# Other PSUM banks for the second weight tile of a down-projection, and one queue for most of the last stores

## The chip, the cores and the metric

The kernel runs on one core of a Trainium2 chip. The core has five engines with a queue each: TensorE (PE, with a separate row PEld for its weight loads), VectorE (DVE), ScalarE (ACT), GpSimd (POOL) and SyncE (SP). TensorE writes its products into PSUM, which has eight banks of 128 x 512 float32 here; VectorE and ScalarE read them from there. Transfers between the main memory and SBUF are issued by SyncE, ScalarE or GpSimd. The metric is the device time of one execution in microseconds (us). The kernel before took 1692.35 us, the median of 3 runs (1691.88 to 1692.66).

## The reference

A decoder trunk of two layers on 512 tokens of width 1024, in float32. Each layer is a half-weighted SwiGLU, a mixer (sliding-window attention beside a short convolution) and a second half-weighted SwiGLU:

```
def swiglu(h, w_gate, w_up, w_down):
    return (jax.nn.silu(h @ w_gate) * (h @ w_up)) @ w_down
...
    for l in range(DEPTH):
        x = x + 0.5 * swiglu(rms_norm(x, ffn1_norm[l]), ffn1_wg[l], ffn1_wu[l], ffn1_wd[l])
        h = rms_norm(x, mix_norm[l])
        z = h @ w_in[l]
...
        x = x + jnp.concatenate([attn_out, conv_out], axis=-1) @ w_out[l]
        x = x + 0.5 * swiglu(rms_norm(x, ffn2_norm[l]), ffn2_wg[l], ffn2_wu[l], ffn2_wd[l])
    return rms_norm(x, final_norm)
```

The inner width of a SwiGLU (D_FF) is 2816, which is eleven blocks of 256 columns.

## The kernel before

**Precision.** Every operand is split into a high and a low part in a shorter float type, and a product is three matmuls: high x high, high x low, low x high. A weight tile arrives as `raw`, ScalarE casts it to `wh` (line 198), and VectorE subtracts to get `wl` (line 199). Where a split is marked "far" (`split_far`, lines 201 to 205), ScalarE writes both `wl = -raw` and `wh`, and a GpSimd transfer adds `raw` to `wl` (line 205), so VectorE has nothing to do with it.

**An FFN in blocks.** `ffn` (from line 758) goes through a list of stages. In three of the four FFNs the list is INNER or LAST: first "p", block 0 done plainly; then "d" for block 0, its down-projection; then "w" for blocks 1, 3, 5 and so on, two blocks at a time by a Winograd-like scheme with seven products instead of eight (`winograd2`, line 861); then "s", the down-projections of most of those blocks by the same scheme (`share`, line 720). The first FFN of the kernel has the list FIRST, which begins with two plain blocks.

**The residual.** The stream x is kept transposed, as eight tiles `xs[c]` of 128 features by 512 tokens. `down` (line 304) yields for each c a sum `acc` in PSUM, and VectorE adds it: `xs[c] += 0.5 * acc` (line 990). Block 0 has two chunks of 128 inner columns, so `abreast` gives 4: one weight tile holds the columns for four c. Of the first weight tile (c = 0 to 3) the four groups are made side by side by `level` (line 290), where `fresh` is set, that is in the three FFNs with the lists INNER and LAST; the last matmuls of its four groups (line 299) follow each other. Of the second weight tile (c = 4 to 7) each group is made on its own by `group` (line 263, matmuls in lines 273, 276 and 280), with six matmuls.

**PSUM banks.** `psum` (line 92) gives out the eight banks under three names: four "mm", two "sc", two "aux". A tile of a name waits until the one that had its bank before has been read. `level` takes all four mm banks, and so does the second weight tile after it. In the Winograd stages, whose seven steps are listed in CHAINS (line 52), the sum x uses mm from step 0 on, w uses aux at step 1, and y uses sc at step 3. Before block 0, sc and aux hold sums of the mixer or of the FFN before, and aux the sum of squares for the norm (line 484). In the last FFN, `Finale.step` (line 1010) turns x back to tokens after the steps 0, 1 and 2 of block 1, through sc, sc, and mm and aux.

**The end.** `Finale.down` (line 1090) makes the last block's down-projection with tokens on the partitions: for each of four token tiles t and two column halves h a product, the residual add (line 1069), the sum of squares on ScalarE (line 1071), and when both halves are in, the inverse root (lines 1077 and 1082, Newton's step in lines 398 to 400). Then `scale` (line 1109) multiplies each half and stores it: h = 1 on VectorE with a store from SyncE's queue, h = 0 on ScalarE with a store from ScalarE's own queue (line 1118). The last token tile's second half is made in two pieces of 256 columns. From token tile 2 on, the order of ScalarE and VectorE is as written (`manual_schedule`, line 1132).

**Order elsewhere.** Where no `manual_schedule` stands, a planner orders each engine's instructions from modelled durations, with the order of the program as priority, and adds the waits.

Of the kernel before, what the change touches and what calls it, by code (L numbers as in the profile page):

```python
# [15 lines left out]
P = 128  # L16
D = 1024
S = 512
# [5 lines left out]
KC = D // P  # L24
NT = S // P
# [33 lines left out]
def trunk_kernel(  # L59
# [23 lines left out]
    nc = tc.nc  # L83
# [8 lines left out]
    def psum(tag, shape, name):  # L92
        return ps.tile(shape, F32, tag=tag, bufs={"mm": 4, "sc": 2, "aux": 2}[tag], name=name)

    def g2(name, dt=F32, shape=(P, S)):
        return work.tile(list(shape), dt, tag="g2", bufs=14, name=name)
# [15 lines left out]
    def small(name, n=NT, dt=F32):  # L112
        return work.tile([P, n], dt, tag="small", bufs=16, name=name)
# [54 lines left out]
    order = []  # L168
# [88 lines left out]
    def take_split():  # L257
        n = state["group"]
        state["group"] += 1
        need_split(n + SPLIT_AHEAD if n else 0)  # L260
        return n, *split_of.pop(n)

    def group(rhs, between=None, own=None, order=range(KC)):

        n, hi, lo = own or take_split()
        acc = psum("mm", [P, S], f"acc_{n}")
        order = order[: len(rhs)]
        first, last = order[0], order[-1]
        late = n in (1, 2, 3)
        for k in order:  # L270
            if between:
                between(k, hi, lo)
            nc.tensor.matmul(acc, hi[:, k, :], rhs[k][0], start=k == first, stop=False)  # L273
            if n == 0:
                nc.tensor.matmul(acc, lo[:, k, :], rhs[k][0], start=False, stop=False)
            nc.tensor.matmul(  # L276
                acc, hi[:, k, :], rhs[k][1], start=False, stop=n == 0 and k == last
            )
            if n != 0 and not late:
                nc.tensor.matmul(acc, lo[:, k, :], rhs[k][0], start=False, stop=k == last)  # L280
        if late:
            for k in order:
                nc.tensor.matmul(acc, lo[:, k, :], rhs[k][0], start=False, stop=k == last)
        return acc

    def abreast(kc):

        return max(1, KC // kc) if kc in (2, 4) else 1

    def level(n, hi, lo, rhs, wide):  # L290

        accs = [psum("mm", [P, S], f"acc_{n}_{j}") for j in range(wide)]
        cols = [slice(j * P, (j + 1) * P) for j in range(wide)]
        for k, (xh, xl) in enumerate(rhs):
            for j in range(wide):
                nc.tensor.matmul(accs[j], hi[:, k, cols[j]], xh, start=k == 0, stop=False)
                nc.tensor.matmul(accs[j], lo[:, k, cols[j]], xh, start=False, stop=False)
            for j in range(wide):
                nc.tensor.matmul(
                    accs[j], hi[:, k, cols[j]], xl, start=False, stop=k + 1 == len(rhs)  # L300
                )
        return accs

    def down(rhs, fresh=False):

        wide = abreast(len(rhs))
        for c in range(0, KC, wide):
            n, hi, lo = take_split()
            if fresh and c == 0:
                yield from enumerate(level(n, hi, lo, rhs, wide))  # L310
                continue
            for j in range(wide):
                cols = slice(j * P, (j + 1) * P)
                yield c + j, group(rhs, own=(f"{n}_{j}", hi[:, :, cols], lo[:, :, cols]))

    def plan():
        def cols(src, k0, kc, n, how=None):
# [84 lines left out]
    class Norm:  # L402
# [65 lines left out]
        def groups(self, n, accs=()):  # L468

            accs = list(accs) or [group(self.h, order=self.order)]  # L470
            parts = self.parts()
            while len(accs) < n:
                at, step = (1, 2) if self.i else (3, 2)
                due = len(accs) == at
                accs.append(
                    group(self.h, lambda k, hi, lo: due and k == step and self.factors(parts))
                )
            return accs
# [279 lines left out]
    def ffn(norm, stages, after=None, late=None):  # L758
# [192 lines left out]
        for i, (what, b) in enumerate(stages):  # L951
# [33 lines left out]
            for c, acc in down(rhs, b == (0,) and not first):  # L985
                if b == (0,):
                    made = {0: "t3", 4: "t1"} if first else {0: "b21", 2: "t2", 5: "t3"}
                    if c in made:
                        norm.make(made[c])
                nc.vector.scalar_tensor_tensor(  # L990
                    xs[c], acc, 0.5, xs[c], op0=ALU.mult, op1=ALU.add
                )
                flush()
                if final:
                    after(c)
# [5 lines left out]
    class Finale:  # L1001
# [88 lines left out]
        def down(self, rhs):  # L1090
            for half in range(2):
                gb = g2(f"gain_{half}")
                nc.sync.dma_start(
                    gb, final_norm[half * S : (half + 1) * S].partition_broadcast(P)
                )
                self.gain.append(gb)
            done = small("done", NT)
            self.widen(0, len(rhs) // 2)
            for t in range(NT):
                rest = done[:, t : t + 1]  # L1100
                acc = self.products(rhs, 0, t, 0, S)
                self.close(acc, 0, t, 0, rest)
                nc.vector.tensor_scalar(rest, rest, 1.0 / D, EPS, op0=ALU.mult, op1=ALU.add)
                if t == 0:
                    self.widen(1, len(rhs) // 2)
            def factor(t, ssq):
                return self.root(t, ssq, done[:, t : t + 1])

            def scale(t, by, h):
                y = self.y[t][h]  # L1110
                if h:
                    nc.vector.scalar_tensor_tensor(
                        y, y, by, self.gain[h], op0=ALU.mult, op1=ALU.mult
                    )
                else:
                    nc.scalar.activation(y, y, AF.Copy, scale=by)
                cols = slice(h * S, (h + 1) * S)
                (nc.sync if h else nc.scalar).dma_start(out[0, t * P : (t + 1) * P, cols], y)

            def piece(t, c0, wide):  # L1120
                ssq = small(f"ssq_end{t}_{c0}", 1)
                self.close(self.products(rhs, 1, t, c0, wide), 1, t, c0, ssq)
                return ssq

            for t in range(NT - 2):
                by = factor(t, piece(t, 0, S))
                for h in (1, 0):
                    scale(t, by, h)


            a, b = NT - 2, NT - 1
            with tc.manual_schedule(engines={act, dve}):
                ssq = piece(a, 0, S)
                early = self.guess(a, ssq, done[:, a : a + 1])
                first = piece(b, 0, H)
                by = self.mend(a, ssq, done[:, a : a + 1], early)
                scale(a, by, 0)
                second = piece(b, H, H)
                scale(a, by, 1)
                rest = done[:, b : b + 1]  # L1140
                nc.vector.scalar_tensor_tensor(
                    rest, first, 1.0 / D, rest, op0=ALU.mult, op1=ALU.add
                )
                by = self.mend(b, second, rest, self.guess(b, second, rest))
                for h in (1, 0):
                    scale(b, by, h)
# [233 lines left out]
```

## Time and profile before

| | |
|---|---|
| median of 3 runs | 1692.35 us |
| profiled execution | 1690.47 us |
| its span, from the first to the last instruction | 1688.6 us |
| granted TensorE clock | 0.999 |
| busy: TensorE, VectorE, ScalarE, GpSimd | 1675.1, 1382.8, 967.7, 215.3 us |
| moved by transfers | 284.19 MB |

The rows come from one profiled execution. A row of the timeline has the start and the duration in us, the engine, the line of the kernel, the operation, the tile written and the tiles read, the shapes, how often the row stands for (x2: two in a row), and in brackets the idle time of the engine before it with what ended it. A matmul of 512 columns is shown with 0.39 us, but the next starts before it ends, so its rate is read from starts. ACTq and SPq are the queues of ScalarE and SyncE; their rows are the issues of transfers.

### The profile page before, as it was taken

How to read it: one execution, taken by the hardware profiler on the slowest of the kernel's cores; microseconds unless marked ns; L12 is line 12 of the kernel's file. 1: busy time of each engine (PE TensorE's matmuls, PEld its weight loads, DVE VectorE, ACT ScalarE, POOL GpSimd, SP SyncE). 2: the span in 40 equal slices, each digit the busy share in tenths (PEclk: the TensorE clock that was granted, in tenths of full speed). 3: DMA queues.
4: the chain of work that ended last, by engine and by line, in shares of the span. 5: the costliest groups of instructions: out<-in, count | busy, mean ns of one | idle time of the engine just before them, and what ended most of it. 6: DMA issues, size and time to landing. Idle time of an engine off the chain costs nothing.

```text
span 1688.6 us, 23567 instructions
## 1 busy us (share of the span) xinstructions
PE 1675.1 (99%) x9014; PEld 1443.3 (85%) x9014; DVE 1382.8 (82%) x1817; ACT 967.7 (57%) x1335; POOL 215.3 (13%) x192
## 2 busy tenths in 40 slices
PE   9999999999999999999999999999999999999998
PEld 6888889988898888889988888999888988888886
DVE  7987679988799967799798677997787997667995
ACT  6545565466566655564465555644555766556654
POOL 1011111001221111111011111110013111111111
PEclk9999999999999999999999999999999999999999
DMA  8467787731597677778466777785226867777881
GB/s 250 104 171 189 186 199 187 188 100 51 135 215 167 174 183 186 187 191 221 150 144 179 187 186 183 198 202 156 63 63 143 219 137 195 184 183 185 224 213 51
DMA packets 191846, 284.19 MB, mean 168 GB/s; under 512 B 9004, under 2 KB 77684, under 8 KB 191732
## 3 DMA queue, kind: packets, MB, share of 16 engines
q1 hardware_dynamic: 151108, 199.95, 37.7%
q0 software_dynamic: 39472, 81.27, 28.6%
q8 instruction: 71, 1.16, 0.3%
q10 hardware_dynamic: 1152, 1.45, 0.2%
q14 instruction: 43, 0.35, 0.1%
HBM read 261.14 MB, written 2.10 MB: 156 GB/s over the span
## 4 chain that ended last, share of the span: by engine, by line
PE 93%; DVE 3%; DMA 2%; issue 1%; POOL 0%; ACT 0%; SPq 0%; ACTq 0%; POOLq 0%; DVEq 0%
PE x L711 25%; PE y L711 12%; PE x_s L696 8%; PE acc L273 7%; PE acc L276 7%; PE acc L280 7%; PE w L711 6%; PE y_s L696 4%; PE x_s L711 3%; PE w_s L696 2%; PE x_m L696 2%; PE at L917 2%; PE y_m L696 1%; PE y_s L711 1%; DMA wl<-raw 1%
## 5 line engine op out<-in xcount | busy, mean ns | idle before, releaser
L198 ACT CAST wh<-raw 128x1024 fp32r<-128x1024 f32 (+1 forms) x482 | 505.2, 1048 | 531.0 <-PE x L711 132.0
L199 DVE TENSOR_TENSOR wl<-raw,wh 128x1024 fp32r<-128x1024 f32 (+1 forms) x481 | 588.4, 1225 | 210.3 <-ACT wh L198 208.3
L273 PE MATMUL acc<-xh,wh 128*128 128x512 f32 x448 | 176.5, 394 | 0.1
L276 PE MATMUL acc<-xl,wh 128*128 128x512 f32 x448 | 175.5, 392 | 0.1
L280 PE MATMUL acc<-xh,wl 128*128 128x512 f32 x416 | 162.5, 391 | 0.0
L193 POOL DMA_DIRECT2D raw<-in_ffn_wu_dram x39 | 47.3, 1217 | 531.6 <-DMA raw<-in_ffn_wu_dram 306.8
L276 PEld LDWEIGHTS acc<-xl,wh 128*128 128x128 f32 x448 | 84.2, 188 | 18.5 <-DVE xl L421 1.7
L273 PEld LDWEIGHTS acc<-xh,wh 128*128 128x128 f32 x448 | 84.2, 188 | 17.1 <-issue 0.5
L280 PEld LDWEIGHTS acc<-xh,wl 128*128 128x128 f32 x416 | 78.1, 188 | 16.2
L193 POOL DMA_DIRECT2D raw<-in_ffn_wg_dram x39 | 47.2, 1249 | 228.0 <-DMA raw<-in_ffn_wu_dram 100.0
L223 DVE TENSOR_TENSOR raw<-raw,raw 128x1024 f32<-128x1024 f32 x58 | 70.9, 1229 | 6.3 <-DMA wl<-raw 5.7
L193 POOL DMA_DIRECT2D raw<-in_ffn_wd_dram x32 | 38.6, 1206 | 260.6 <-DMA raw<-in_ffn_wd_dram 142.4
L711 PE MATMUL w<-wh,fb21h 128*128 128x512 f32 x152 | 60.7, 399 | 0.0
L711 PE MATMUL x<-wh,ft2h 128*128 128x512 f32 x152 | 60.6, 398 | 0.0
L711 PE MATMUL y<-wh,ft3h 128*128 128x512 f32 x152 | 60.4, 398 | 0.0
L711 PE MATMUL w<-wl,fb21h 128*128 128x512 f32 x152 | 59.4, 391 | 0.0
L711 PE MATMUL x<-wl,ft2h 128*128 128x512 f32 x152 | 59.3, 390 | 0.0
L711 PE MATMUL y<-wh,ft3l 128*128 128x512 f32 x152 | 59.2, 390 | 0.0
L711 PE MATMUL y<-wl,ft3h 128*128 128x512 f32 x152 | 59.2, 390 | 0.0
L711 PE MATMUL w<-wh,fb21l 128*128 128x512 f32 x152 | 59.2, 389 | 0.0
L711 PE MATMUL x<-wl,fb11h 128*128 128x512 f32 x152 | 59.2, 389 | 0.0
L711 PE MATMUL x<-wh,fb11h 128*128 128x512 f32 x152 | 59.1, 389 | 0.0
(503 smaller groups left out, 4805.0 us busy)
## 6 DMA issues: line engine op xcount, KB each, us to landing
raw<-in_ffn_wu_dram SPq DMA_DIRECT2D x127, 512.0 KB, 4.3
raw<-in_ffn_wd_dram SPq DMA_DIRECT2D x104, 512.0 KB, 5.0
raw<-in_ffn_wg_dram SPq DMA_DIRECT2D x87, 512.0 KB, 5.0
raw<-in_ffn_wu_dram POOLq DMA_DIRECT2D x39, 512.0 KB, 8.0
raw<-in_ffn_wg_dram POOLq DMA_DIRECT2D x39, 512.0 KB, 6.0
raw<-in_w_in_dram SPq DMA_DIRECT2D x36, 512.0 KB, 3.6
raw<-in_ffn_wd_dram POOLq DMA_DIRECT2D x32, 512.0 KB, 8.4
raw<-raw POOLq DMA_DIRECT2D x20, 512.0 KB, 7.2
```

The source lines that it names most:

```text
L193: nc.gpsimd.dma_start(out=r, in_=rows_of(*more), accum_op=ALU.add)
L198: nc.scalar.copy(hi, raw)
L199: eng.tensor_sub(lo, raw, f32(hi))
L223: nc.vector.tensor_add(a11, a11, s1)
L273: nc.tensor.matmul(acc, hi[:, k, :], rhs[k][0], start=k == first, stop=False)
L276: nc.tensor.matmul(acc, hi[:, k, :], rhs[k][1], start=False, stop=n == 0 and k == last)
L280: nc.tensor.matmul(acc, lo[:, k, :], rhs[k][0], start=False, stop=k == last)
L696: nc.tensor.matmul(accs[c // 2][:, c % 2, :], w[:, k, cols], x_[:, 2 * h + k, :], start=start and c % 2 == 0 and h + k + i == 0, stop=h + ...
L711: nc.tensor.matmul(accs[u], x_[:, 2 * h + k, tok], w[:, k, :], start=start and h + k + i == 0, stop=h + k == 2 and i == 2, skip_group_chec ...
L917: nc.tensor.transpose(tp[:, t * P : (t + 1) * P], ups[t][:, c * P : (c + 1) * P], ident)
```

## The change

The groups of the second weight tile (c = 4 to 7) of block 0, in the FFNs where the first weight tile goes through `level`, write to the banks sc, sc, aux and aux in place of the four mm banks. And at the end the h = 0 stores of the token tiles 0 to 2 are issued by SyncE in place of ScalarE; the last token tile's stays with ScalarE.

```
-    def group(rhs, between=None, own=None, order=range(KC)):
+    def group(rhs, between=None, own=None, order=range(KC), tag="mm"):
 
         n, hi, lo = own or take_split()
-        acc = psum("mm", [P, S], f"acc_{n}")
+        acc = psum(tag, [P, S], f"acc_{n}")
...
                 cols = slice(j * P, (j + 1) * P)
-                yield c + j, group(rhs, own=(f"{n}_{j}", hi[:, :, cols], lo[:, :, cols]))
+                own = (f"{n}_{j}", hi[:, :, cols], lo[:, :, cols])
+                tag = ("sc", "sc", "aux", "aux")[j] if fresh else "mm"
+                yield c + j, group(rhs, own=own, tag=tag)
...
                 cols = slice(h * S, (h + 1) * S)
-                (nc.sync if h else nc.scalar).dma_start(out[0, t * P : (t + 1) * P, cols], y)
+                queue = nc.scalar if h == 0 and t == NT - 1 else nc.sync
+                queue.dma_start(out[0, t * P : (t + 1) * P, cols], y)
```

## The prediction

> **What bounds the kernel now.** I read the page's engine table first.
>
> ```profile
> span 1688.6 us, 23567 instructions
> PE 1675.1 (99%) x9014; PEld 1443.3 (85%) x9014; DVE 1382.8 (82%) x1817; ACT 967.7 (57%) x1335; POOL 215.3 (13%) x192
> ```
>
> TensorE works 1675.1 of 1688.6 us, so 13.5 us in all is idle, the start and the tail included. A change that leaves the matmuls alone can only win from those 13.5 us. The waits of TensorE come next, first those of the matmuls, then those of the weight loads (columns: total us, times, longest).
>
> ```profile
> PE acc L273 <- DVE x L990: 1.9, 3, 0.7
> PE x_m L696 <- DVE wl L199: 0.9, 2, 0.5
> PEld acc L273 <- DVE x L990: 3.2, 3, 1.1
> ```
>
> The longest wait of the matmuls is on the line that the change touches: a group's first matmul (L273) waits for the residual add that empties its bank (L990), three times, once for each of the three FFNs whose block 0 goes through `level`. The timeline of TensorE at the three places shows what one wait costs.
>
> ```profile
> 538.25 1.07 PE L299 MATMUL acc<-a,wh 128*128 128x512 f32 x4
> 540.00 0.50 PE L273 MATMUL acc<-a,wh 128*128 128x512 f32 x1 [0.68 <-DVE x L990]
> 540.34 0.39 PE L276 MATMUL acc<-a,wh 128*128 128x512 f32 x1
> ...
> 874.29 1.07 PE L299 MATMUL acc<-a,wh 128*128 128x512 f32 x4
> 875.92 0.50 PE L273 MATMUL acc<-a,wh 128*128 128x512 f32 x1 [0.56 <-DVE x L990]
> ...
> 1372.84 1.07 PE L299 MATMUL acc<-a,wh 128*128 128x512 f32 x4
> 1374.59 0.50 PE L273 MATMUL acc<-a,wh 128*128 128x512 f32 x1 [0.68 <-DVE x L990]
> ```
>
> Four matmuls take 1.07 us and one 0.39, so they start (1.07 - 0.39) / 3 = 0.227 us apart. Unhindered, L273 would start at 538.25 + 4 x 0.227 = 539.16 and L276 at 539.39; L276 starts at 540.34. The first wait costs 0.95 us: 0.84 of delay and 0.11 because the restarted matmul takes 0.34 to its successor instead of 0.227. The second costs 875.92 - 875.20 + 0.11 = 0.83, the third 1374.59 - 1373.75 + 0.11 = 0.95. **Together 2.73 us**, between the 1.9 and the 3.2 of the two wait lists.
>
> **Part one: the banks.** No instruction is added or removed; groups 4 to 7 of the down-projection write sc, sc, aux, aux instead of waiting for the four mm banks. The old tenants of those banks (the mixer's sums in both, then the squared sum in aux, all read while the block's own products run) are gone by then, so the wait falls away. What is late next? VectorE and two transfers, which do not come earlier because TensorE does.
>
> ```profile
> 538.00:567.00 29.00, 28.32 (x125) 23.12 (x124) 28.97 (x32) 17.91 (x21) 1.21 (x1) 1.00 0.51 123
> ...
> 565.78 2.35 DVE L199 TENSOR_TENSOR wl<-raw,wh 128x1024 fp32r<-128x1024 f32 x2
> 568.45 1.23 DVE L199 TENSOR_TENSOR wl<-raw,wh 128x1024 fp32r<-128x1024 f32 x1 [0.31 <-ACT wh L198]
> ...
> 567.57 0.19 PEld L711 LDWEIGHTS x<-wl,ft1h 128*128 128x128 f32 x1
> ```
>
> The first row is the window after the first wait: length, then busy time of PE, PEld, DVE. VectorE is busy 28.97 of 29.00 us, so it cannot deliver sooner than it does now. The split that it makes last in this stretch (the first of two, done at 565.78 + 1.22 = 567.00) is loaded at 567.57: 0.57 us of room. TensorE, 0.95 us earlier, would run into it and keep about 0.57. (The signal costs some hundredths and the quicker restart after a wait gives 0.11 back; I let them cancel.) The other splits of that stretch have over 1.1 us of room, by the same subtraction.
>
> ```profile
> 872.56 1.42 POOL L205 DMA_DIRECT2D wl<-raw  x1
> DMA to landing us min/median/max: 8.6/8.6/8.6
> 881.73 0.19 PEld L711 LDWEIGHTS x<-wl,fb11h 128*128 128x128 f32 x1
> ...
> 1369.87 0.90 POOL L205 DMA_DIRECT2D wl<-raw  x1
> DMA to landing us min/median/max: 7.6/7.6/7.6
> 1380.39 0.19 PEld L711 LDWEIGHTS x<-wl,fb11h 128*128 128x128 f32 x1
> ```
>
> At the second place the limit is the weight whose low part is made by a transfer. It is issued at 872.56, before the wait, and lands 8.6 us later at 881.16; the load is at 881.73. Again 0.57 us of room against a gain of 0.83, so about 0.57 is kept. At the third place the same transfer lands at 1369.87 + 7.6 = 1377.47 and is loaded at 1380.39: 2.9 us of room. VectorE's splits have about as much there, since the final stage's transposes stretch TensorE's steps, so the whole 0.95 is kept. Sum: 0.57 + 0.57 + 0.95 = **2.1 us** kept. The ends: with the room as it stands or smaller by a tenth for rounding, 1.9; with nothing in the way, 2.73. I take 2.1, because both rooms are read from rows. Right behind, VectorE idles again and waits for ScalarE's cast (the row of 568.45), and the casts and the loads wait for buffers that TensorE frees, so what is kept travels to the end.
>
> The new tenants must leave in time too.
>
> ```profile
> 545.67 1.88 DVE L990 SCALAR_TENSOR_TENSOR x<-acc,x 128x512 f32<-128x512 f32 x3
> ...
> 551.18 5.44 PE w L711 x24
> ```
>
> The last add of the eight ends at 545.67 + 1.88 = 547.55. The next user of the aux banks is w, from 551.18 (550.2 if TensorE is 0.95 earlier): 2.7 us of cover. The next user of the mm banks, x, finds them emptied earlier than before.
>
> A rule of the Trainium skill speaks against a gain here: the page "TensorE: Matmul & The Clock Gate", section "HAM oscillation — how this bites in real kernels", reports of a thin-M kernel that double-buffering PSUM on top of a better loop order gave no further gain. By it this part would be worth 0 and the sum would be the tail's alone; by the row at 540.00 TensorE waits for nothing but a bank there, and I go by the row.
>
> **Part two: the stores.** Three issues move from ScalarE's queue to SyncE's; the last token tile's stays. The first two are not on the chain. The third is (chain of waits, then VectorE's timeline, then the last issue and the landing of the last two stores).
>
> ```profile
> 1681.36 0.73 ACT ytok L1116
> 1682.11 0.34 ACTq L1118
> 1682.50 0.52 ACT ysq L1071 x2
> 1683.04 0.30 ACT r_end L1077
> ...
> 1681.68 0.42 DVE L1069 SCALAR_TENSOR_TENSOR ytok<-end,ytok 128x256 f32<-128x256 f32 x1 [0.41 <-PE end L1062]
> 1682.68 0.15 DVE L1141 SCALAR_TENSOR_TENSOR done<-ssq_end,done 128x1 f32<-128x1 f32 x1
> ...
> 1684.76 0.34 ACTq L1118 DMA_DIRECT2D out_dram<-ytok  x1
> DMA to landing us min/median/max: 2.3/2.6/2.9
> ```
>
> The square of the last half tile (1682.50) starts when ScalarE is through with the issue of 0.34 us. Its input is ready at 1681.68 + 0.42 = 1682.10 and ScalarE's scaling ends at 1682.09. Without the issue it starts near 1682.14, 0.36 earlier. VectorE's small operation of 1682.68 is done by 1682.83, before the new end of r_end (1682.98), so it doesn't take the place of the issue. Both last stores start **0.36 us** earlier. SyncE gets three issues of 0.34 us more; its queue has no loads any more, the moved store is ready at 1682.1 and the next at 1682.8, the last one at 1684.4, so they don't meet. Bounds: 0 if a store in the same queue held up the last one by as much, 0.36.
>
> **Sum.** 2.1 + 0.36 = 2.5 us. The profiled execution took 1690.47 us (span 1688.6 and 1.9 around it) and would take 1688.0; the median of the runs, 1692.35, lies 1.88 above it. **1692.35 - 2.5 = 1689.9 us**, with its own range 1689.1 (2.73 + 0.36 and a little) to 1690.4. About 0.2%, 3.4 us, is what a measurement here can tell from no change: below 1689.0 is faster, above 1695.7 slower.
>
> **The rivals.** *The order changes, for the better.* VectorE's, ScalarE's and TensorE's order is planned from modelled times; with groups 4 to 7 ready about a microsecond sooner, the plan after each of the three places may come out otherwise. If it moves the tight split forward, the 2.73 come whole; if it also saves the mixer's waits (0.9 us in the second list), 2.73 + 0.36 + 0.9 = 4.0 and the time is 1688.4. For it: at 538 work for later stages stands ahead of the adds, so the plan does move things. Against it: the adds already stand in the program's own order.
>
> *Nothing of part one arrives.* If the room at each place is nil, because VectorE or the transfers come later by what TensorE comes earlier, only the tail's 0.36 is left: 1692.0. For it VectorE's 28.97 of 29.00; against it the rooms of 0.57, 0.57 and 2.9.
>
> *The new banks become the wait (slower).* The mm banks no longer press for the adds of groups 6 and 7, and the plan may put other VectorE work ahead of them. The place is w's first matmul, and it decides when the last add ends after 550.2, that is from three operations of 1.13 us (2.35 - 1.22 in the row of 565.78) ahead of it on (3.4 against 2.7 us of cover). With six (6.8 us) the add ends at 554.3 and TensorE waits 4.1 us, 3.1 more than was won: 3 x 3.1 - 0.4 = 9 us, 1701.4. With four it is about 0.9 x 3 - 0.4, 1694.7. Against it: the adds precede that work in the program.
>
> *It doesn't do what it says:* the final stage's transposes use sc and aux too, but a step later, behind adds that are done by then; I see no place for it.
>
> **The numbers.** Forecast 0.53; better order 0.25, mostly beyond 0.2%; nothing arrives 0.10; new wait 0.12, nearly all of it slower. So faster 0.25, same 0.64, slower 0.11. The range runs from the better order's 1688.2 to 1692.6, past the time at which nothing arrives; the new wait lies outside, and a part of the better order.
>
> **What would show it.** Right: the wait lists have no row L273 <- L990; L273 follows L299 at 0.227 us; a wait of some 0.3 us appears at the load of wl for ft1h in the first FFN, and one at the first load of wl for fb11h in the second; none in the third; ScalarE's queue has one store, and ysq follows VectorE's L1069 by 0.04. Wrong: a wait of w or y on L990, a matmul of the final stage waiting on an add, or the tail from TensorE's last matmul to the end longer than 1688.6 - 1681.6 = 7.0 us (6.6 expected).

## The result and the profile after

| | before | after |
|---|---|---|
| median of 22 runs each | 1691.87 us | 1688.66 us |
| lowest and highest | 1690.70, 1697.94 us | 1687.96, 1690.39 us |
| profiled execution, its span | 1690.47, 1688.6 us | 1690.13, 1688.4 us |
| granted TensorE clock | 0.999 | 0.999 |

The ratio of the times is 0.9979, with an interval from 0.9973 to 0.9986: the kernel became about 3.5 us faster by the ratio, 2.4 to 4.6 us by the ends of its interval. The medians lie 3.21 us apart and the lowest times 2.74 us.

The two profiled executions do not show that at first sight. The engine table of the changed kernel has the span and the busy times:

```profile
span 1688.4 us, 23574 instructions
...
PE 1674.9 (99%) x9014; PEld 1443.3 (85%) x9014; DVE 1382.3 (82%) x1817; ACT 968.1 (57%) x1335; POOL 215.2 (13%) x192
```

TensorE is idle for 1688.4 - 1674.9 = 13.5 us, as long as before. The profiled execution of the changed kernel lies 1.5 us above its median, while that of the kernel before is 1.4 us below its own. So the gain has to be looked for place by place, not in the spans. The waits of TensorE, matmuls and then weight loads (columns: total us, times, longest), tell what has changed:

```profile
PE x L713 <- DMA wl<-raw: 1.5, 1, 1.5
...
PEld x L713 <- DMA wl<-raw: 1.9, 1, 1.9
```

The row L273 <- L990 (L992 now) is gone from both lists; a wait of x for a transfer is new, once, 1.5 us. The timeline of TensorE at the three places of the old wait:

```profile
539.27 1.07 PE L299 MATMUL acc<-a,wh 128*128 128x512 f32 x4
540.18 0.39 PE L273 MATMUL acc<-a,wh 128*128 128x512 f32 x1
...
874.38 1.07 PE L299 MATMUL acc<-a,wh 128*128 128x512 f32 x4
875.28 0.39 PE L273 MATMUL acc<-a,wh 128*128 128x512 f32 x1
...
880.95 0.39 PE L713 MATMUL x<-wh,fb11l 128*128 128x512 f32 x1
882.86 0.50 PE L713 MATMUL x<-wl,fb11h 128*128 128x512 f32 x1 [1.52 <-DMA wl<-raw]
883.20 0.39 PE L713 MATMUL x<-wh,fb11h 128*128 128x512 f32 x1
...
1373.58 1.07 PE L299 MATMUL acc<-a,wh 128*128 128x512 f32 x4
1374.49 0.39 PE L273 MATMUL acc<-a,wh 128*128 128x512 f32 x1
```

L273 now starts 0.91, 0.90 and 0.91 us after the first of the four L299, which is four matmuls at 0.227: nothing is in its way. Against the same rows before, the three gaps shrank by 0.84, 0.73 and 0.84 us, and the slow restart of 0.11 fell away three times. What happened to that gain right behind each place is told with the first experiment and with the prediction's steps. The row of 882.86 is the new wait.

The end of the kernel, first ScalarE's timeline, then VectorE's:

```profile
1681.12 0.72 ACT L1118 ACTIVATE ytok<-ytok,y_end 128x512 f32<-128x512 f32 x1
1681.90 0.42 ACT L1073 ACTIVATE ysq<-ytok 128x256 f32<-128x256 f32 x1
...
1682.69 0.30 ACT L1079 ACTIVATE r_end<-ssq_end,done 128x1 f32<-128x1 f32 x1 [0.28 <-DVE done L1144]
```

```profile
1681.45 0.42 DVE L1071 SCALAR_TENSOR_TENSOR ytok<-end,ytok 128x256 f32<-128x256 f32 x1 [0.42 <-PE end L1064]
1681.79 0.74 DVE L1114 SCALAR_TENSOR_TENSOR ytok<-ytok,y_end,gain 128x512 f32<-128x512 f32 x1
1682.45 0.15 DVE L1144 SCALAR_TENSOR_TENSOR done<-ssq_end,done 128x1 f32<-128x1 f32 x1
```

The store is gone from ScalarE, and the square `ysq` starts right behind the scaling, 0.45 us after VectorE's last add has begun; before, it started 1682.50 - 1681.68 = 0.82 after it. But `r_end`, which comes next, now waits 0.28 us for `done`: its bias. VectorE writes `done` (L1144) behind a scaling of 0.74 us (L1114).

### The profile page after: what moved, and what is told of

It reads as the page before. It is cut to its first block, busy times and chain, and to the rows that moved or that the text cites. A ratio compares the mean times of both kernels' runs of the same rounds, so it can differ in the third digit from the quotient of the medians.

```text
span 1688.4 us, 23574 instructions
## 1 busy us (share of the span) xinstructions
PE 1674.9 (99%) x9014; PEld 1443.3 (85%) x9014; DVE 1382.3 (82%) x1817; ACT 968.1 (57%) x1335; POOL 215.2 (13%) x192
## 4 chain that ended last, share of the span: by engine, by line
PE 91%; DMA 3%; DVE 3%; issue 2%; POOL 1%; ACT 0%; SPq 0%; POOLq 0%; DVEq 0%; ACTq 0%
PE x L713 25%; PE y L713 12%; PE x_s L698 8%; PE acc L276 6%; PE w L713 6%; PE acc L273 6%; PE acc L280 6%; PE y_s L698 4%; PE x_s L713 3%; PE w_s L698 2%; PE x_m L698 2%; PE at L919 2%; DMA wl<-raw 2%; PE y_m L698 1%; PE y_s L713 1%
## 5 line engine op out<-in xcount | busy, mean ns | idle before, releaser
L273 PE MATMUL acc<-xh,wh 128*128 128x512 f32 x448 | 176.6, 394 | 0.1
L276 PE MATMUL acc<-xl,wh 128*128 128x512 f32 x448 | 175.4, 392 | 0.1
L193 POOL DMA_DIRECT2D raw<-in_ffn_wu_dram x39 | 47.2, 1215 | 536.1 <-DMA raw<-in_ffn_wu_dram 330.4
L276 PEld LDWEIGHTS acc<-xl,wh 128*128 128x128 f32 x448 | 84.2, 188 | 18.6 <-DVE xl L423 1.6
L273 PEld LDWEIGHTS acc<-xh,wh 128*128 128x128 f32 x448 | 84.2, 188 | 17.4 <-issue 0.5
L193 POOL DMA_DIRECT2D raw<-in_ffn_wg_dram x39 | 47.2, 1246 | 224.1 <-DVE raw L223 75.9
L193 POOL DMA_DIRECT2D raw<-in_ffn_wd_dram x32 | 38.6, 1205 | 257.9 <-DMA raw<-in_ffn_wd_dram 153.2
L713 PE MATMUL x<-wl,ft1h 128*128 128x512 f32 x152 | 59.2, 389 | 0.0
```

Of the source, the lines that this page charges most:

```text
L193: nc.gpsimd.dma_start(out=r, in_=rows_of(*more), accum_op=ALU.add)
L276: nc.tensor.matmul(acc, hi[:, k, :], rhs[k][1], start=False, stop=n == 0 and k == last)
L713: nc.tensor.matmul(accs[u], x_[:, 2 * h + k, tok], w[:, k, :], start=start and h + k + i == 0, stop=h + k == 2 and i == 2, skip_group_chec ...
```

## The experiments

Each experiment ran with the kernel before on the same chip. Ratios are against that kernel. A run of the kernel before on those chips gave medians of 1692.31 (runs 1 to 4), 1691.71 (5, 6, 7, 9) and 1691.88 us (8, 10).

**1. The banks without the stores.** The changed kernel with the stores as they were:

```
-                queue = nc.scalar if h == 0 and t == NT - 1 else nc.sync
-                queue.dma_start(out[0, t * P : (t + 1) * P, cols], y)
+                (nc.sync if h else nc.scalar).dma_start(out[0, t * P : (t + 1) * P, cols], y)
```

> Only the four groups' banks change; the stores stay as before. Theory (the banks carry the gain, the stores some 0.1 us): the three waits of L273 on L990 are gone, and the time is 2 to 3 us below the kernel before (ratio 0.9982 to 0.9988), about 0.1 us above the full change. In the profile each of the three places gives 0.8 to 0.95 us, and what is taken back is taken back at the first load of wl for fb11h in the second FFN, by as much as the transfer into wl lands late in that execution. Tail: from the start of TensorE's last matmul to r_end 1.68 us, as before. Rival (the stores are worth 0.36 us or more): 0.4 us or more above the full change.

Median 1688.81 us, ratio 0.9982 (0.9973 to 0.9991). This is the cleanest trace for part one, since no transfer was late in it. The timeline of TensorE at the three places:

```profile
539.03 1.07 PE L299 MATMUL acc<-a,wh 128*128 128x512 f32 x4
...
874.14 1.07 PE L299 MATMUL acc<-a,wh 128*128 128x512 f32 x4
...
1371.94 1.07 PE L299 MATMUL acc<-a,wh 128*128 128x512 f32 x4
```

and its weight loads behind them:

```profile
568.80 0.19 PEld L713 LDWEIGHTS x<-wl,ft1h 128*128 128x128 f32 x1
...
880.72 0.19 PEld L713 LDWEIGHTS x<-wl,fb11h 128*128 128x128 f32 x1
...
1378.52 0.19 PEld L713 LDWEIGHTS x<-wl,fb11h 128*128 128x128 f32 x1
```

An execution can be early or late as a whole when it comes to a place; here it was 539.03 - 538.25 = 0.78 us later than the execution before at the first. What a place yields is the change of that difference between the row ahead of the wait and a row behind everything that could take the gain back. The ninth load of x in the first FFN is at 568.80, and at 568.93 in the kernel before (the row is shown with the prediction's steps): 0.13 earlier, so 0.78 + 0.13 = 0.91 is kept. In the second FFN the difference goes from 874.14 - 874.29 = -0.15 to 880.72 - 881.73 = -1.01: 0.86 kept. In the third from 1371.94 - 1372.84 = -0.90 to 1378.52 - 1380.39 = -1.87: 0.97. **Together 2.74 us**, all that the three waits cost. At TensorE's last matmul the difference is 1679.48 - 1681.36 = -1.88, so 0.78 + 1.88 = 2.66 us of it reaches the end of the kernel: between the three places nothing else of note was won or lost in this trace.

**2. The stores without the banks.** The kernel before with the three lines of the new queue.

> Only the queue of three stores changes; the banks stay as before. Theory: ysq starts 0.36 us earlier, but r_end, which reads the value that VectorE's L1141 writes, waits for it, so from the start of TensorE's last matmul (1681.36 before) to r_end 1.56 us instead of 1.68: a gain of 0.12 us, which no interval will tell from nothing. All three waits of L273 on L990 are there. Rival (the issue of 0.34 us was the whole price): 1.32 us to r_end, a gain of 0.36.

Median 1692.39 us, ratio 1.0 (0.9991 to 1.0008): nothing that can be measured. Its waits of TensorE:

```profile
PE acc L273 <- DVE x L990: 1.9, 3, 0.7
...
PE x L711 <- DMA wl<-raw: 1.2, 1, 1.2
```

and the last `r_end` in ScalarE's timeline:

```profile
1683.49 0.72 ACT L1116 ACTIVATE ytok<-ytok,y_end 128x512 f32<-128x512 f32 x1
...
1685.06 0.30 ACT L1077 ACTIVATE r_end<-ssq_end,done 128x1 f32<-128x1 f32 x1 [0.28 <-DVE done L1142]
```

Two things follow. The wait of x for the transfer is here with the old banks, so it does not need the new ones. And `r_end` waits for `done` as in the changed kernel: from the start of TensorE's last matmul (1683.49 in that trace) to `r_end` it takes 1.57 us, against 1683.04 - 1681.36 = 1.68 before. Part two is worth 0.1 us at this point, not 0.36.

**3. The factor before the scaling.** In the changed kernel the statement that writes `rest` (the column of `done`) goes ahead of the scaling and the second piece:

```
                 by = self.mend(a, ssq, done[:, a : a + 1], early)
+                rest = done[:, b : b + 1]
+                nc.vector.scalar_tensor_tensor(
+                    rest, first, 1.0 / D, rest, op0=ALU.mult, op1=ALU.add
+                )
                 scale(a, by, 0)
                 second = piece(b, H, H)
                 scale(a, by, 1)
-                rest = done[:, b : b + 1]
-                nc.vector.scalar_tensor_tensor(
-                    rest, first, 1.0 / D, rest, op0=ALU.mult, op1=ALU.add
-                )
```

> The full change, and VectorE's L1141 (the small sum for the last token tile's root) stands ahead of the scaling of token tile 2 instead of behind it. Theory: r_end follows ysq at once, 1.32 us after the start of TensorE's last matmul instead of 1.56: 0.24 us below the full change. Rival (r_end waits for something else, or L1141 in its new place delays L1069): 1.5 us or more.

Median 1689.09 us, ratio 0.9986 (0.9977 to 0.9995). VectorE's timeline, then ScalarE's:

```profile
1679.13 0.16 DVE L1141 SCALAR_TENSOR_TENSOR done<-ssq_end,done 128x1 f32<-128x1 f32 x1
1679.56 0.42 DVE L1071 SCALAR_TENSOR_TENSOR ytok<-end,ytok 128x256 f32<-128x256 f32 x1 [0.27 <-PE end L1064]
```

```profile
1680.56 0.29 ACT L1079 ACTIVATE r_end<-ssq_end,done 128x1 f32<-128x1 f32 x1
```

`done` is written before the last add begins, and `r_end` has no wait. From the start of the last matmul (1679.24) it takes 1.32 us, which is 1.68 less 0.36: the whole gain of the store, once the other predecessor is out of the way. It also shows in the tail, from the end of the last matmul to the end of the span: 6.96 to 7.04 us in the three profiles with the old stores (the kernel before, runs 1 and 5), 6.92 to 6.99 in the six with the new stores and the late `done` (the changed kernel, runs 2, 4, 6, 8 and 9), and 6.68 to 6.70 in the three where `done` is early (runs 3, 7 and 10). In the time of the kernel a quarter of a microsecond is not visible: the interval is over ten times as wide, and the median came out no lower than that of run 1 on the same chip.

**4. The far transfer first.** The transfer that x waited for is L205, which adds `raw` to `wl` (the split marked "far"). It stands in GpSimd's queue behind L193, another adding transfer, which makes the sum of two weight tiles for the Winograd scheme. In this experiment L193 is ordered behind L205 in the first pair of blocks of the three FFNs; nothing else is changed:

```
-                nc.gpsimd.dma_start(out=r, in_=rows_of(*more), accum_op=ALU.add)
+                with tc.issue_after(state["far"]) if "far" in state else nullcontext():
+                    nc.gpsimd.dma_start(out=r, in_=rows_of(*more), accum_op=ALU.add)
...
-        nc.gpsimd.dma_start(out=f32(lo), in_=raw, accum_op=ALU.add)
+        return nc.gpsimd.dma_start(out=f32(lo), in_=raw, accum_op=ALU.add)
...
-                split_far(hi, lo, raw)
+                add = split_far(hi, lo, raw).ins
+                if isinstance(order[n][1], tuple) and how == "alone":
+                    state["far"] = add
...
```

> The full change, and in the three blocks the transfer that adds into wl (L205) stands ahead of the accumulating load L193 in GpSimd's queue; L193 waits for an earlier load to land, and L205 behind it with it. Theory (what the second FFN takes back is L205 held up behind L193): L205 is issued within 1 us of the end of L203 in each of the three FFNs, the load of wl for fb11h waits in none, and the time is 0 to 1.5 us below the full change, with less spread between executions. Rival (the landing is late because the transfer itself takes 8 us, not because it is issued late): the wait stays, above 0.5 us, or L193, issued later, makes a wait elsewhere and the time doesn't fall.

Median 1688.84 us, ratio 0.9979 (0.997 to 0.9988). GpSimd's timeline in the second FFN, in the changed kernel with the landing of its L205 behind it:

```profile
873.91 1.21 POOL L193 DMA_DIRECT2D raw<-in_ffn_wg_dram  x1 [6.34 <-DMA raw<-in_ffn_wu_dram]
874.63 1.42 POOL L205 DMA_DIRECT2D wl<-raw  x1
...
DMA to landing us min/median/max: 8.2/8.2/8.2
```

and in this experiment (the lines are one further down):

```profile
872.25 0.86 POOL L206 DMA_DIRECT2D wl<-raw  x1 [4.57 <-DVE sums L536]
872.80 1.54 POOL L194 DMA_DIRECT2D raw<-in_ffn_wg_dram  x1
...
DMA to landing us min/median/max: 5.0/5.0/5.0
```

In the changed kernel GpSimd stands for 6.34 us at L193, which waits for a load to land, and L205 comes 0.72 us behind it, though ScalarE had written its input by 870.80 + 1.05 = 871.85, 2.8 us before L205 was issued. With the order turned round, L205 is issued 2.4 us earlier in this execution and lands 5.0 us later instead of 8.2: at 877.25 instead of 882.83. x waits for no transfer any more. The median did not fall below the changed kernel's 1688.66 us. Against the kernel before on its own chip it is 3.47 us lower, the changed kernel's 3.21; the intervals do not separate the two, so it is not shown that a typical execution has the wait.

**5. The same order in the kernel before.** The edit of run 4, with the old banks and stores.

> The kernel before (mm banks, stores as before), with the transfer into wl ahead of the accumulating load L193 in GpSimd's queue in the three blocks. Theory (the late landing is a wait of its own that some executions have with either set of banks, and that is not what the banks bring): no wait of x on a transfer into wl; the three waits of L273 on L990 stand as before; the median is 0 to 0.8 us below the kernel before. Rival (the old banks hide the late landing, it costs only with the new ones): no change at all, and no less spread.

Median 1691.31 us, ratio 0.9997 (0.9989 to 1.0006). The waits have the old row in full (three lines further down), and none on the transfer:

```profile
PE acc L276 <- DVE x L993: 1.9, 3, 0.7
```

So ordering the transfer is no substitute for the banks. Its 11 times reach from 1690.69 to 1692.06 us, the 35 of the kernel before on this chip from 1690.66 to 1694.05: the low end stays, the high end comes down. Runs 4 and 5 differ by the banks and the stores, and ran on two chips. Against the kernel before on its own chip, run 4 is 1692.31 - 1688.84 = 3.47 us faster and run 5 is 1691.71 - 1691.31 = 0.40, so the banks and the stores together make 3.1 us by the medians; the traces have 2.74 and 0.12.

**6. Two new banks.** Only the first two groups of the second weight tile leave the mm banks:

```
-                tag = ("sc", "sc", "aux", "aux")[j] if fresh else "mm"
+                tag = ("sc", "sc", "mm", "mm")[j] if fresh else "mm"
```

> The full change, but only the first two groups of the second weight tile get new banks (sc, sc); the other two stay in mm. Theory (only the first of the four groups waits for a bank): no wait of L273 on L990, the same 0.8 to 0.95 us at each place, the time equal to the full change. Rival (all four banks count, since the adds of groups 0 and 1 come late for groups 6 and 7): a wait of 0.2 us or more before the third group and part of the 2.7 us lost.

Median 1689.48 us, ratio 0.9987 (0.9978 to 0.9996), and no wait of a group on L992 in the lists. By the time the third group begins, twelve matmuls or 12 x 0.227 = 2.7 us later, the adds have emptied mm. So the wait hangs on the first two groups at most. With the aux banks left alone the kernel is still faster than the kernel before; by the medians it is 0.8 us slower than the changed kernel, which the intervals do not separate. In its profile x waits 1.1 us for the far transfer.

**7. Everything together.** The changed kernel with the edits of runs 3 and 4.

> The full change with both additions: L1141 early, and the transfer into wl ahead of L193. Theory: neither wait (r_end on done, x on the transfer into wl) is left, 0.24 us from the tail for certain and up to 1 us in the executions where the transfer landed late; median 0 to 1 us below the full change. Rival: the interval shows nothing, since most executions have no late landing.

Median 1688.48 us, ratio 0.9981 (0.9972 to 0.999). Neither the wait of x nor that of `r_end` is left in its trace. Two of its twelve times, 3920.73 and 6968.44 us, lie far outside. The ratio leaves them out, and without them the median is 1688.39 us. No trace shows where that time went, and run 10, the same kernel, has nothing like it in 11 executions.

**8. The changed kernel again,** unedited, and **10. run 7 again,** both on one chip.

> The changed kernel once more, to see which of its waits return. Theory: no wait of L273 on L990 and r_end waiting 0.28 us for done, in this execution as in the first; the wait of 1.5 us on the transfer into wl in the second FFN is a matter of the single execution and need not return; without it the span is 1686 to 1687 us. Rival (the wait belongs to the new banks): it returns with 1 us or more, and the span is 1688 or more.

> The full change with both additions once more, on the same chip as the changed kernel. Theory: 0.2 to 0.6 us below the changed kernel, 0.24 of it from the tail, and the slowest executions nearer to the median. Rival: no difference that the intervals show.

The changed kernel: median 1688.75 us, ratio 0.9986 (0.9978 to 0.9995). Everything together: 1688.19 us, 0.9979 (0.997 to 0.9988). The waits of TensorE in the changed kernel's new trace have the row of the transfer again:

```profile
PE x L713 <- DMA wl<-raw: 1.3, 1, 1.3
```

This is the sign of the rival: the wait returns with over 1 us and the span is 1688.4 us. That the new banks alone are its cause is excluded by run 2, which has it with the old banks, and by runs 1 and 3, which have the new banks and not the wait. That it comes more often or lasts longer with the new banks, since TensorE reaches this place 0.84 us sooner, is not excluded.

In the other trace ScalarE's last steps run without a wait:

```profile
1680.22 0.72 ACT L1121 ACTIVATE ytok<-ytok,y_end 128x512 f32<-128x512 f32 x1 [0.15 <-DVE y_end L405]
...
1681.54 0.30 ACT L1082 ACTIVATE r_end<-ssq_end,done 128x1 f32<-128x1 f32 x1
```

This version has the lowest median of all and beats the kernel before; that it beats the changed kernel, by 0.56 us in the medians, is likely from its trace (1.32 against 1.56 us from the last matmul to `r_end`, and no late transfer) but not shown by the intervals, which overlap. Its slowest execution took 1689.20 us, that of the changed kernel on this chip 1693.00.

**9. The first group back in mm.** The reverse of run 6: the first group of the second weight tile waits for a mm bank, the others have new ones:

```
-                tag = ("sc", "sc", "aux", "aux")[j] if fresh else "mm"
+                tag = ("mm", "sc", "sc", "aux")[j] if fresh else "mm"
```

> The full change, but the first group of the second weight tile stays in mm and the other three get new banks (sc, sc, aux). Theory (only the first group waits): the three waits of L273 on L990 are back, 1.9 us in the list of the matmuls, and the time is that of the kernel before (ratio 0.999 to 1.001). Rival (the gain comes from the new order of VectorE's and TensorE's work or from the freed mm banks for x): 1 us or more below the kernel before.

Median 1690.62 us, ratio 0.9996 (0.9987 to 1.0005): not to be told from the kernel before. TensorE's timeline in the first FFN:

```profile
540.21 0.39 PE L273 MATMUL acc<-a,wh 128*128 128x512 f32 x1
540.44 0.39 PE L276 MATMUL acc<-a,wh 128*128 128x512 f32 x1
541.05 0.50 PE L273 MATMUL acc<-a,wh 128*128 128x512 f32 x1 [0.22 <-DVE x L992]
```

The wait came back, but in part: the planner put two matmuls of the second group, whose bank is free, ahead of the first group, so the first group meets its bank later. The lists have 0.4 us of matmuls and 1.6 of weight loads on L992, against 1.9 and 3.2 before. From L276 to the late L273 it is 0.61, 0.50 and 0.61 us in the three FFNs where it would be 0.227; with the slow restart of 0.11 each that costs 0.49, 0.38 and 0.49, together 1.4 us of the 2.73. The median is 1.1 us under that of the kernel before on this chip. So the theory's 1.9 us in the list did not come, the rival's "1 us or more" did by the medians, and the interval tells neither from no change; in the trace half of the price comes back when the first group stays in mm.

Its profile also has the longest wait of x for the far transfer, 2.1 us, and what follows it is in no other trace:

```profile
884.10 0.79 PE L713 MATMUL x<-wl,fb11h 128*128 128x512 f32 x1 [2.07 <-DMA wl<-raw]
884.69 0.63 PE L713 MATMUL x<-wh,fb11h 128*128 128x512 f32 x1
885.12 0.63 PE L713 MATMUL x<-wh,fb11l 128*128 128x512 f32 x1
```

The matmuls start 0.43 us apart. The eight from 884.10 on take 3.51 us, where eight at 0.227 take 1.82, and the granted clock is 0.57 between 884 and 888 us; in the changed kernel, after its wait of 1.52 us, it is 1.00 between 882 and 886. So here the late transfer costs 2.2 us of delay and 1.7 more behind it, and the profiled execution took 1693.99 us. In the runs with the old order of the transfers and new banks (the changed kernel, runs 1, 3, 6, 8 and 9), the seven executions above 1691.5 us have a mean granted clock of 0.997 or 0.998, all others 0.999 or 1.0; runs 4 and 10, with the far transfer first, have no execution above 1691.5. Only one of the seven has a trace, so that the others had the same wait is likely, not shown.

## Why the prediction was right, and where it was not

**The mechanism of part one was right.** The three waits fell away, TensorE ran from L299 into L273 at 0.227 us, and the time followed from the banks alone (run 1) and not from the stores (run 2). The forecast of 1689.9 us lay 1.2 us above the result, whose 1688.66 us is in the range; the ratio sits on the bound of what can be told from no change, on the side that had a chance of 0.25.

**The term of 2.1 us was mis-sized: 2.74 arrived.** Of 0.57 + 0.57 + 0.95 the last was right (0.97). The other two were caps, and both fell for one reason: a room read from one execution and one order was taken as fixed.

In the first FFN the cap was about right for the order before. The weight loads of the kernel before around the tight split:

```profile
567.12 0.19 PEld L711 LDWEIGHTS x<-wh,ft1h 128*128 128x128 f32 x1
567.35 0.19 PEld L711 LDWEIGHTS x<-wh,ft1l 128*128 128x128 f32 x1
...
568.93 0.19 PEld L711 LDWEIGHTS x<-wl,ft1h 128*128 128x128 f32 x1
```

and those of the changed kernel:

```profile
567.15 0.19 PEld L713 LDWEIGHTS x<-wh,ft1h 128*128 128x128 f32 x1
567.38 0.19 PEld L713 LDWEIGHTS x<-wh,ft1l 128*128 128x128 f32 x1
567.61 0.19 PEld L713 LDWEIGHTS x<-wh,ft1h 128*128 128x128 f32 x1
567.97 0.19 PEld L713 LDWEIGHTS x<-wl,ft1h 128*128 128x128 f32 x1 [0.18 <-DVE wl L199]
...
569.01 0.19 PEld L713 LDWEIGHTS x<-wl,ft1h 128*128 128x128 f32 x1
```

The load of `wl` was third and is fourth now: the planner moved a load of `wh` ahead of it. Unhindered it would be at 567.61 + 0.23 = 567.84 and it is at 567.97; of this 0.13 the quicker successor (0.11 instead of 0.23) gives back 0.12. The wait that the prediction placed here is there, 0.18 instead of 0.3 us, and costs about nothing. This is near the prediction's rival of a better order, in its first half ("the 2.73 come whole"), which had 0.25: that rival moved the split forward, and here the load of its result moved back. What was said against it, that the program's order would hold, was about VectorE's adds and not about TensorE's own loads. What the old order would have kept was not run. An estimate from these rows: this execution is 1.02 us later than the one before at the first place (539.27 - 538.25) and would be 0.04 later at the third load (567.61 - 567.57), so 0.98 less the delay of 0.36 for a load due at 567.61 and made at 567.97, with 0.12 of it given back: about 0.7 us.

In the second FFN the transfer was taken to land at 881.16 whatever TensorE does. In run 1 it was issued at 872.30 and landed 8.2 us later, at 880.50; that is 0.66 us earlier than in the trace before, and the load came at 880.72 with no wait. In the changed kernel's profile it landed at 882.83. There x was late by 1.79 us: its predecessor starts at 880.95, so it was due at 881.18 and started at 882.86, and the restart cost 0.11 more. That is more than the 0.84 us won at this place, and what makes it late is the place behind L193: run 2 has the wait with the old banks, run 4 removes it with the new ones. Of the eight profiles with the old order of the transfers, five show matmuls of x waiting for it in the second FFN (1.1 to 2.1 us, the changed kernel twice) and three do not (the kernel before, runs 1 and 3). The two groups differ in how long GpSimd stood at L193 for its load: 6.20 to 6.62 us in the five and 4.24 to 4.37 in the three. Why that load lands sooner in some executions is open. The profiled executions of the changed kernel took 1690.13 and 1690.18 us, 1.4 to 1.5 above the medians, and of the 22 times of the changed kernel all but two lie under 1689.5.

**The term of 0.36 us at the end was over-sized: 0.12 at `r_end`.** The step that failed is the sentence that VectorE's small operation "doesn't take the place of the issue". The sum compared its end, 1682.83, with the new end of `r_end`; it had to be compared with the new start, 1683.04 - 0.36 = 1682.68, since `r_end` reads `done` as its bias. It was 0.15 late, and the signal came on top. The square follows the add as predicted; the chain of waits then goes through VectorE's scaling and `done`. From the last matmul to `r_end` it is 1.68 before and 1.56 after, 1.57 in run 2, and 1.32 in run 3 where `done` was early. Nor was the tail 6.6 us: from the last matmul's end, 1681.13 + 0.28 = 1681.41, to 1688.4 it is 7.0, as before, for the last store was issued in 0.38 us instead of 0.34 and took 3.0 to land instead of 2.9. In that one execution nothing of the 0.12 reached the end; over the profiles listed with run 3 the new stores shorten the tail by some hundredths on their own and by 0.3 with the early `done`.

**The level.** The median of the kernel before was 1692.35 in three runs and 1691.87 in 22, which lowers the forecast by 0.48. With that, 0.64 more for part one and 0.24 less for part two, the sum is 1689.0 us, 0.35 above the measured median; the two errors of size partly cancel, which was luck. **That 0.35 stays open.** The lowest times differ by 2.74, and 2.74 + 0.12 = 2.86 lies in the interval of 2.4 to 4.6. More late transfers in the kernel before would explain it, and run 5, whose median is 0.4 under that of the kernel before on the same chip, fits; but its interval includes no change, and only profiled executions show the transfer.

**The other rivals.** No new bank became a wait: no matmul of w or y and none of the final stage waits on an add. "Nothing of part one arrives" is ruled out by run 1. The finding of the Trainium skill that was weighed (the page "TensorE: Matmul & The Clock Gate", section "HAM oscillation — how this bites in real kernels": no further gain from double-buffering PSUM in a thin-M kernel) does not carry over to this kernel: its banks gave 2.74 us in the trace of run 1 and a ratio of 0.9982 on their own.

## What to carry to other kernels

When a bank, a buffer or a queue is freed, first list every other operand of the instruction that was held up, and compare the time at which each is ready with the new start of that instruction, not with its end. A room between a transfer's landing and its use is a sample from one execution; a planner's order is as little fixed as that room, so a cap read from one trace is a bound for the range, not the likeliest value. Where two profiled executions differ by less than their medians do, compare the same instructions on both sides of each place instead of the spans.

## What the runs showed of the hardware

After a wait of TensorE of 2.07 us the granted clock was 0.57 over the 4 us from 884 to 888 (run 9); after one of 1.52 us it stayed at 1.00 (the changed kernel). Each was seen once, and where the bound lies was not measured.

The same adding transfer, L205 of the second FFN, landed 7.7 to 9.0 us after its issue in the eight profiles where it stands behind L193 (8.2 in the changed kernel), and 5.0 to 7.1 us after it in the four where it stands ahead (5.0 in run 4, 7.1 in run 5, 5.4 in run 7 and 5.5 in run 10). GpSimd's queue kept its order while L193 stood for its load: 6.34 us in the changed kernel, 4.37 in the kernel before, and 6.62 in run 2, with L205 0.72 us behind L193 in all three. GpSimd's timeline of the kernel before (its L205 at 872.56 stands in the prediction):

```profile
871.84 1.21 POOL L193 DMA_DIRECT2D raw<-in_ffn_wg_dram  x1 [4.37 <-DMA raw<-in_ffn_wu_dram]
```

and that of run 2:

```profile
875.02 1.21 POOL L193 DMA_DIRECT2D raw<-in_ffn_wg_dram  x1 [6.62 <-DMA raw<-in_ffn_wu_dram]
875.74 1.42 POOL L205 DMA_DIRECT2D wl<-raw  x1
```

The Trainium skill says on the page "DMA: Bandwidth & Descriptors", section "SWDGE vs HWDGE vs iDMA", that a transfer which accumulates per element can be issued by GpSimd only. No run here tried another queue; by that rule L193 and L205 have to stay in GpSimd's queue, where run 4 changed their order.
